# Delta-rule sequences: a 64x64 map per chunk made ahead of the chain, outputs taken from whole pairs

## The chip, the cores and the metric

The kernel runs on one core of a Trainium2 chip. The metric is the device time of one execution in microseconds (us), the median of three runs. The core has a matrix engine (TensorE, PE in the profile, with PEld for its weight loads), a vector engine (VectorE, DVE), an activation engine (ScalarE, ACT), GpSimd (POOL) and a queue that issues transfers (SyncE, SP). [...]

## The reference, cut to what matters

The program is a trunk of four layers over 1024 tokens with 1024 channels: gated convolution, diagonal state space, RWKV-7 time mixing, gated convolution. Only the third layer is touched. There, each of 16 heads carries a 64x64 state that is updated token by token:

```python
def _rwkv_step(state, inp):
    r_t, w_t, k_t, v_t, kk_t, a_t = inp
    sa = jnp.einsum("bhvk,bhk->bhv", state, -kk_t)
    state = (state * w_t[:, :, None, :] + sa[..., None] * (kk_t * a_t)[:, :, None, :]
             + v_t[..., None] * k_t[:, :, None, :])
    out = jnp.einsum("bhvk,bhk->bhv", state, r_t)
    return state, out
```

The outputs are normalised per head, get a bonus term, are gated by silu(z) and go through `w_out`.

## The kernel before, in words

**Tiling.** The layer treats the tokens in two halves of 512 (`h`), and the channels in eight blocks of 128 (`m`), two heads to a block. A unit is one pair (m, h): two heads, 512 tokens, eight chunks of 64 tokens. All large products (`sp`, `op`, lines 326 to 328) are split into three products of 128x128 by 128x512.

**The parts of a unit.** `use_k` and `use_r` turn the products for k and r into scaled tiles. `prep` (line 1960) makes the 64x64 products inside each chunk (`s`, line 1982), transposes the keys (`kbtp`, `kbt`) and makes the values that do not need the state (`wps`, into `uv`). `tsolve` (line 2024) inverts the unit triangular 64x64 system of each chunk on VectorE alone, in eight steps of three instructions (`tv` line 2048, `td` line 2053, `ti` line 2054). `join` (line 2057) completes the inverse (`tt`) with small products (`zp`, `tp`) and multiplies it into the keys (`a2`, line 2097). `seq` (line 2105) is the chain over the eight chunks:

- the bank `p1` is opened with `tt` times `uv` (line 2122), 16 small products a unit;
- for each chunk, one 128x128 product of the state with `ra` (line 2131) gives both this chunk's correction (64 rows) and, in the other 64 rows, the part of its outputs that the old state makes;
- ScalarE copies the correction into `uv` (line 2132);
- a second 128x128 product with `kbt` (line 2137) gives the update, of which VectorE uses the two diagonal 64x64 blocks, one instruction each (line 2140);
- after four chunks the outputs are completed with `scr` (line 2147) and copied into `o` (line 2150).

Then the outputs are normalised, transposed (`otp`, line 2176) and stored.

**What sets the order.** `rwkv_layer` writes units m = 0 to 7 of a half one after the other. Unit m's own k and r work is interleaved, by generators, with `tsolve` of unit m-1 and `seq` of unit m-2. A scheduler that knows priorities (`PS`, `PT`, `PJ` for `seq`, `tsolve` and `join`/`prep`) then fixes each engine's order. Behind the eighth unit of the first half come two products for z of the second half, the second half's small products (`pwa`, line 1640) and its z and v work; behind the eighth unit of the second half comes the output product (`op`). In these two places there is no next unit, and the last `tsolve`, `join` and `seq` have less beside them.

The state tile is 128x128 with zeros off the diagonal blocks. In `paux`, two PSUM banks under the name `aux` serve all short products; `pseq` holds one bank `sq` and two `p1`.

Of the kernel before, what the change touches and what calls it, by code (L numbers as in the profile page):

```python
# [15 lines left out]
P = 128  # L16
# [1581 lines left out]
def rwkv_layer(S, X, bg, l, last, nxt):  # L1598
# [9 lines left out]
    dST = dram_list(S, "dST", [P, P])  # L1608
# [313 lines left out]
def inner_setup(S, rg, T_):  # L1922
# [179 lines left out]

    gn, bn = S.vec[("lnx_g",)], S.vec[("lnx_b",)]

    def seq(m, h, R, dVT, dST, dBV, dZ, dY):
        st = rg.tile([P, P], F32, tag="state", name="state", bufs=2)
        if h == 0:
            G.memset(st, 0.0)
        else:
            nc.sync.dma_start(st, dST[m][:])  # L2110
        ot = rg.tile([P, HT], F32, tag="o", name="o", bufs=2)
        o4 = ot.rearrange("p (c s) -> p c s", c=4)

        def bank(ph):

            p1 = S.pseq.tile([P, 2, 2, P], F32, tag="p1", name="p1", bufs=2)
            nc.tensor.matmul(p1[:, 0, 0, 0:2], S.ident, zero, start=True, stop=False, skip_group_check=True)
            for c2 in range(2):
                for hd in range(2):
                    for w in range(2):  # L2120
                        rb, cs = rows_b[w], slice(hd * 64, hd * 64 + 64)
                        nc.tensor.matmul(p1[rb, w, c2, cs], R.tt[rb, 2 * (2 * ph + c2) + hd, :],
                                         R.uv[w][rb, 2 * ph + c2, cs], start=False, stop=False, skip_group_check=True)
            return p1
        p1s = [bank(0)]
        for c in range(8):
            w, c2, ph = c % 2, c // 2, c // 4
            rb = rows_b[w]
            uv = R.uv[w][:, c2, :]
            p1 = p1s[ph][:, w, c2 % 2, :]  # L2130
            nc.tensor.matmul(p1, R.ra[:, c, :], st, start=False, stop=False, skip_group_check=True)  # L2131
            SC.copy(uv[rb, :], p1[rb, :])  # L2132
            yield
            if c == 2:
                p1s.append(bank(1))
            p2 = sq("p2")
            last = nc.tensor.matmul(p2[:, 0:P], R.kbt[c // 4][:, c % 4, :], uv, start=True, stop=True)  # L2137
            for hd in range(2):
                cs = slice(hd * 64, hd * 64 + 64)
                V.scalar_tensor_tensor(st[cs, cs], st[cs, cs], R.pc[cs, c:c + 1], p2[cs, cs], ALU.mult, ALU.add)  # L2140
            if c % 4 == 3:
# [7 lines left out]
                for w in range(2):  # L2149
                    SC.copy(o4[rows_k[w], 2 * ph:2 * ph + 2, :], p1s[ph][rows_k[w], w])  # L2150
# [62 lines left out]
```

## Time and profile before

| what | value |
|---|---|
| median of three runs | 2815.74 us (2814.3 to 2817.0) |
| the profiled execution's own time | 2819.03 us |
| its span | 2817.1 us |
| PE, PEld busy | 2673.0 us (95%), 2119.2 us (75%) |
| DVE, ACT, POOL busy | 2009.8 us (71%), 1168.8 us (41%), 644.9 us (23%) |
| mean granted TensorE clock | 0.966 |
| instructions | 40692 |

The span is the time from the first to the last profiled instruction; the execution's own time is 1.9 us longer. A busy PE counts each product from its start to its modelled end, and products overlap; how many PE can do in a microsecond is read from the distance between starts, not from the busy share. Line numbers such as L2140 are those of the kernel before; in the changed kernel the lines from 2103 on are new.

### The profile page before, as it was taken

To read this page: it belongs to the slowest core of one execution; us is meant where nothing else is said; L and a number is where in the kernel's file an instruction comes from. 1 tells how busy PE (TensorE), PEld (TensorE's weight loads), DVE (VectorE), ACT (ScalarE), POOL (GpSimd) and SP (SyncE) were. 2 spreads that over 40 slices of the span, in tenths; PEclk is the share of its full clock that TensorE was granted. 3 is DMA by queue.
4 is the path that set the end of the run, shared out by engine and by line. 5 is a ranking of instruction groups with operands and counts; after the bars stand their busy time and mean duration, and the time that the engine had idled before them with its cause. 6 is when DMAs were issued, how large, how long until landed. Compare 5 with 4: busy or idle time off the path is not lost.

```text
span 2817.1 us, 40692 instructions
## 1 busy us (share of the span) xinstructions
PE 2673.0 (95%) x14939; PEld 2119.2 (75%) x14939; DVE 2009.8 (71%) x3584; ACT 1168.8 (41%) x2243; POOL 644.9 (23%) x696
## 2 busy tenths in 40 slices
PE   8999999999999999899899899888889999999998
PEld 6887888778887878677677567666668777887887
DVE  6787865477657446887887776888866678877544
ACT  3333332242135223666565475555433343224332
POOL 1143422221115132203243110333222211111000
PEclk9999999999999999999996799999799999999999
DMA  5333321347774233473222245223324433324511
GB/s 169 99 97 98 94 76 58 92 146 211 217 237 157 90 101 102 134 227 120 77 95 91 60 163 168 76 85 93 100 91 135 139 115 116 101 72 131 172 64 38
DMA packets 463129, 331.56 MB, mean 118 GB/s; under 512 B 49449, under 2 KB 398929, under 8 KB 462929
## 3 DMA queue, kind: packets, MB, share of 16 engines
q1 hardware_dynamic: 462928, 328.96, 38.5%
q8 instruction: 118, 1.93, 0.3%
q14 instruction: 83, 0.67, 0.1%
HBM read 250.77 MB, written 77.59 MB: 117 GB/s over the span
## 4 chain that ended last, share of the span: by engine, by line
PE 71%; DVE 15%; issue 4%; ACT 4%; DMA 3%; POOL 3%; SPq 0%; DVEq 0%; POOLq 0%; ACTq 0%
PE op L327 3%; PE op L326 3%; PE op L328 3%; PE gp L328 3%; PE gp L327 3%; PE gp L326 3%; PE sp L326 2%; PE sp L327 2%; PE sp L328 2%; PE qa L506 2%; PE qa L507 2%; PE qa L508 2%; DVE tv L2048 2%; PE zp L326 2%; PE zp L328 2%
## 5 line engine op out<-in xcount | busy, mean ns | idle before, releaser
L299 DVE TENSOR_TENSOR wl<-wraw,wh 128x1024 fp32r<-128x1024 f32 x255 | 332.6, 1304 | 217.0 <-ACT wh L298 213.5
L298 ACT CAST wh<-wraw 128x1024 fp32r<-128x1024 f32 x255 | 267.4, 1049 | 519.0 <-PE gp L327 185.9
L905 POOL TENSOR_TENSOR ln_s<-ln_s,rp 128x512 f32<-128x512 f32 x42 | 60.3, 1435 | 209.9 <-DVE rp L901 209.9
L2140 DVE SCALAR_TENSOR_TENSOR state<-state,pc,p 64x64 f32<-64x64 f32 x256 | 70.8, 277 | 39.7 <-PE p L2137 35.5
L2048 DVE TENSOR_TENSOR tv<-ti,mi 128x128 f32<-128x128 f32 (+3 forms) x128 | 97.1, 759 | 2.5
L2131 PE MATMUL p<-state,ra 128*128 128x128 f32 x256 | 65.2, 341 | 31.3 <-DVE state L2140 31.0
L2131 PEld LDWEIGHTS p<-state,ra 128*128 128x128 f32 x256 | 45.2, 213 | 54.8 <-DVE state L2140 49.2
L2132 ACT COPY uv<-p 64x128 f32<-64x128 f32 x128 | 33.3, 260 | 122.2 <-PE p L2131 121.0
L920 POOL TENSOR_TENSOR rp<-r_0h,r_0l 128x512 f32<-128x512 f32 x24 | 36.5, 1548 | 180.9 <-PE op L327 180.2
L328 PE MATMUL gp<-r_0h,wl 128*128 128x512 f32 x192 | 77.2, 402 | 0.0
L327 PE MATMUL gp<-r_0l,wh 128*128 128x512 f32 x192 | 76.8, 400 | 0.0
L326 PE MATMUL gp<-r_0h,wh 128*128 128x512 f32 x192 | 76.6, 399 | 0.0
L326 PE MATMUL gp<-r_1h,wh 128*128 128x512 f32 x192 | 76.4, 398 | 0.0
L328 PE MATMUL gp<-r_1h,wl 128*128 128x512 f32 x192 | 76.0, 396 | 0.2 <-DVE wl L299 0.2
L327 PE MATMUL gp<-r_1l,wh 128*128 128x512 f32 x192 | 75.5, 393 | 0.0
L2137 PE MATMUL p<-uv,kbt 128*128 128x128 f32 x256 | 66.2, 344 | 8.7 <-ACT uv L2132 8.6
L1982 PE MATMUL s<-ra,kb 64*128 64x128 f32 x512 | 71.6, 302 | 1.0 <-ACT scr L1988 0.9
L2137 PEld LDWEIGHTS p<-uv,kbt 128*128 128x128 f32 x256 | 44.9, 210 | 36.6 <-ACT uv L2132 31.3
L1982 PEld LDWEIGHTS s<-ra,kb 64*128 64x128 f32 x512 | 61.3, 202 | 13.4 <-ACT scr L1988 2.9
L1991 POOL TENSOR_TENSOR scr<-scr,mask 128x512 f32<-128x512 f32 x32 | 45.9, 1435 | 70.2 <-ACT scr L1988 70.0
L327 PE MATMUL sp<-xs0l,wh 128*128 128x512 f32 x128 | 55.0, 430 | 1.9 <-DVE xs0l L195 1.9
L1710 POOL COPY pc<-pt 128x8 f32<-128x8 f32 x16 | 5.5, 342 | 222.0 <-ACT pt L1707 222.0
(851 smaller groups left out, 8734.7 us busy)
## 6 DMA issues: line engine op xcount, KB each, us to landing
wraw<-in_conv_w_in_dram SPq DMA_DIRECT2D x84, 512.0 KB
wraw<-in_rwkv_w_rkvz_dram SPq DMA_DIRECT2D x64, 512.0 KB
wraw<-in_ple_gate_dram SPq DMA_DIRECT2D x56, 512.0 KB
wraw<-in_conv_w_out_dram SPq DMA_DIRECT2D x24, 512.0 KB
xt<-xd SPq DMA_DIRECT2D x48, 256.0 KB
wraw<-in_ssm_w_in_dram SPq DMA_DIRECT2D x21, 512.0 KB
xd<-rp SPq DMA_DIRECT2D x40, 256.0 KB
wraw<-in_rwkv_w_out_dram SPq DMA_DIRECT2D x16, 512.0 KB
```

What stands on the lines that cost most here:

```text
L298: nc.scalar.copy(wh, raw)
L299: nc.vector.tensor_tensor(wl, raw, f32(wh[:]), ALU.subtract)
L326: nc.tensor.matmul(ps, lh, xh, start=(n == 0), stop=False)
L327: nc.tensor.matmul(ps, lh, xl, start=False, stop=False)
L328: nc.tensor.matmul(ps, ll, xh, start=False, stop=(n == kt - 1))
L506: nc.tensor.matmul(ps, wh[:, k0 + k, :], xh, start=first and k == 0, stop=False, skip_group_check=True)
L905: nc.gpsimd.tensor_tensor(s, s, rs, ALU.add)
L1982: nc.tensor.matmul(pss[hd][:, c * P:(c + 1) * P], kb[rows, 2 * c + w, :], ra[rows, 2 * c + w, :], start=True, stop=True)
L2048: V.tensor_tensor(tv, ti[:, b:8, 4 * b:4 * b + 4].unsqueeze(2).to_broadcast([P, n, c, 4]), mi[:, 4 * b:4 * b + 4, 0:c].rearrange("p q c -> ...
L2131: nc.tensor.matmul(p1, R.ra[:, c, :], st, start=False, stop=False, skip_group_check=True)
L2137: last = nc.tensor.matmul(p2[:, 0:P], R.kbt[c // 4][:, c % 4, :], uv, start=True, stop=True)
L2140: V.scalar_tensor_tensor(st[cs, cs], st[cs, cs], R.pc[cs, c:c + 1], p2[cs, cs], ALU.mult, ALU.add)
```

## The change

`join` gets two more stages. The inverse `tt` is also multiplied into the transposed keys (`at`) and into the values (`u0`), and the result is multiplied with `kbt` (`gt`): a 64x64 map of each chunk and head, kept where `ant` stood. In `seq` all eight chunks' updates that do not need the state are accumulated into one bank `pd` beforehand (line 2145); a chunk of the chain is then one 64x64 product for each head with the state (line 2151) and one VectorE instruction over both heads (line 2153). The state after every chunk is kept (`sv`, 9 x 64 columns, 128 partitions). The products with `ra` (line 2169, K = 64, 64 columns, one for each head and chunk) now only feed the bank `p1`, which is opened with an identity product of `uv` (line 2164); the corrections are copied into `uv` four times a unit, and the outputs are completed with `scr` (line 2182) for the whole unit at once. The transposes at the end (`otp`) take an `aux` bank.

```diff
-    dST = dram_list(S, "dST", [P, P])
+    dST = dram_list(S, "dST", [P, CH])
...
+        pa, pu = aux("at"), aux("u0")
+        for dst, src in ((pa, lambda w, c2, cs: an[rows_b[w], c2, cs]),
+                         (pu, lambda w, c2, cs: R.uv[w][rows_b[w], c2, cs])):
+            for c2 in range(4):
+                for hd in range(2):
+                    for w in range(2):
+                        rb, cs = rows_b[w], slice(hd * 64, hd * 64 + 64)
+                        nc.tensor.matmul(dst[rb, c2 * P + hd * 64:c2 * P + hd * 64 + 64], tt[rb, 2 * c2 + hd, :],
+                                         src(w, c2, cs), start=True, stop=True)
+        SC.copy(R.ant, pa)
+        for w in range(2):
+            SC.copy(R.uv[w][rows_b[w]].rearrange("p a b -> p (a b)"), pu[rows_b[w], :])
+        yield
+        pg = [aux("gt"), aux("gt")]
+        for c2 in range(4):
+            for hd in range(2):
+                for w in range(2):
+                    rb, cs = rows_b[w], slice(hd * 64, hd * 64 + 64)
+                    nc.tensor.matmul(pg[w][cs, c2 * CH:(c2 + 1) * CH], an[rb, c2, cs],
+                                     R.kbt[c2 // 2][rb, (2 * c2 + w) % 4, cs], start=True, stop=True)
+        for w in range(2):
+            SC.copy(R.ant[:, w * 256:(w + 1) * 256], pg[w][:, 0:256])
+        yield
...
-        st = rg.tile([P, P], F32, tag="state", name="state", bufs=2)
+        sv = rg.tile([P, 9, CH], F32, tag="state", name="state", bufs=2)
...
-            nc.tensor.matmul(p1, R.ra[:, c, :], st, start=False, stop=False, skip_group_check=True)
-            SC.copy(uv[rb, :], p1[rb, :])
-            yield
-            if c == 2:
-                p1s.append(bank(1))
-            p2 = sq("p2")
-            last = nc.tensor.matmul(p2[:, 0:P], R.kbt[c // 4][:, c % 4, :], uv, start=True, stop=True)
-            for hd in range(2):
-                cs = slice(hd * 64, hd * 64 + 64)
-                V.scalar_tensor_tensor(st[cs, cs], st[cs, cs], R.pc[cs, c:c + 1], p2[cs, cs], ALU.mult, ALU.add)
...
+        pd = sq("pd")
+        clear(pd[:, 0:2])
+        for c in range(8):
+            for cs in heads:
+                nc.tensor.matmul(pd[cs, c * CH:(c + 1) * CH], R.kbt[c // 4][:, c % 4, cs], R.uv[c % 2][:, c // 2, cs],
+                                 start=False, stop=False, skip_group_check=True)
+        gt = R.ant.rearrange("p (w c k) -> p w c k", w=2, c=4)
+        yield
+        for c in range(8):
+            for cs in heads:
+                nc.tensor.matmul(pd[cs, c * CH:(c + 1) * CH], gt[cs, c % 2, c // 2, :], sv[cs, c, :],
+                                 start=False, stop=True, skip_group_check=True)
+            V.scalar_tensor_tensor(sv[:, c + 1, :], sv[:, c, :], R.pc[:, c:c + 1], pd[:, c * CH:(c + 1) * CH],
+                                   ALU.mult, ALU.add)
             yield
...
+        for w in range(2):
+            for hd in range(2):
+                nc.tensor.matmul(p1[hd][rows_b[w], :, w, :], S.ident[rows_b[w], rows_b[w]], R.uv[w][rows_b[w], :, heads[hd]],
+                                 start=False, stop=False, skip_group_check=True)
+        yield
+        for c in range(8):
+            for hd in range(2):
+                nc.tensor.matmul(p1[hd][:, c // 2, c % 2, :], R.ra[heads[hd], c, :], sv[heads[hd], c, :],
+                                 start=False, stop=False, skip_group_check=True)
...
+        for w in range(2):
+            for hd in range(2):
+                SC.copy(R.uv[w][rows_b[w], :, heads[hd]], p1[hd][rows_b[w], :, w, :])
+        yield
+        for c2 in range(4):
+            for hd in range(2):
+                for w in range(2):
+                    nc.tensor.matmul(p1[hd][rows_k[w], c2, w, :], R.scr[w][:, c2, hd, :], R.uv[w][:, c2, heads[hd]],
+                                     start=False, stop=True, skip_group_check=True)
+        for w in range(2):
+            for hd in range(2):
+                SC.copy(o4[rows_k[w], :, heads[hd]], p1[hd][rows_k[w], :, w, :])
...
-        ps = sq("otp")
+        ps = aux("otp")
```

How the engines' orders move is shown at three places. In these rows a name is the tile written, then the tiles read; a row's last number is the shape written, and a product that stands once in the order is two rows of the profile.

First, PE in the middle of a unit of the second half (unit 4), with the chain of an earlier unit in it. Before, one chunk after the other:

```order
L1759 MATMUL pb<-kpl,c_ones_r 128x512
L2131 MATMUL p_17709<-state,ra 128x128
L328 MATMUL sp<-xs0h,wl 128x512
L326 MATMUL sp<-xs0h,wh 128x512
L2137 MATMUL p_17762<-uv,kbt 128x128
L1982 MATMUL s_17964<-ra,kb 128x128 x4
L327 MATMUL sp<-xs0l,wh 128x512
L2131 MATMUL p_17709<-state,ra 128x128
L328 MATMUL sp<-xs0h,wl 128x512
L326 MATMUL sp<-xs0h,wh 128x512
L2137 MATMUL p_17768<-uv,kbt 128x128
L2147 MATMUL p_17709<-uv,scr 64x64 x8
```

Now, in the same unit:

```order
L2151 MATMUL pd<-state,ant 64x64 x2
L2169 MATMUL p_18475<-state,ra 128x64
L2169 MATMUL p_18476<-state,ra 128x64
L327 MATMUL sp<-xs1l,wh 128x512
L328 MATMUL sp<-xs1h,wl 128x512
L2151 MATMUL pd<-state,ant 64x64 x2
L2169 MATMUL p_18475<-state,ra 128x64
L2169 MATMUL p_18476<-state,ra 128x64
L326 MATMUL sp<-xs1h,wh 128x512
L2151 MATMUL pd<-state,ant 64x64 x2
```

A chunk was two products with two or three large ones after each; it is now four smaller ones in two shapes, with one or two large ones after them, and all eight chunks stand within some 40 rows.

Second, VectorE at the same place. Before, the two state updates of a chunk stand between the steps of `tsolve`:

```order
L2048 TENSOR_TENSOR tv<-ti,mi 128x288
L1735 TENSOR_TENSOR kk<-kk,prn 128x512
L2140 SCALAR_TENSOR_TENSOR state<-state,pc,p_17269 64x64 x2
L2053 TENSOR_REDUCE td<-tv 128x72
L1738 TENSOR_TENSOR kb<-kk,ga 128x4x2x64
L2054 TENSOR_TENSOR ti<-ti,td 128x3x24
L2048 TENSOR_TENSOR tv<-ti,mi 128x320
L2140 SCALAR_TENSOR_TENSOR state<-state,pc,p_17304 64x64 x2
L2053 TENSOR_REDUCE td<-tv 128x80
```

Now they stand close together behind most of `tsolve`:

```order
L2048 TENSOR_TENSOR tv<-ti,mi 128x128
L2153 SCALAR_TENSOR_TENSOR state<-state,pc,pd 128x64
L2053 TENSOR_REDUCE td<-tv 128x32
L2054 TENSOR_TENSOR ti<-ti,td 128x8x4
L2153 SCALAR_TENSOR_TENSOR state<-state,pc,pd 128x64 x2
L1735 TENSOR_TENSOR kk<-kk,prn 128x512
L2153 SCALAR_TENSOR_TENSOR state<-state,pc,pd 128x64
L1738 TENSOR_TENSOR kb<-kk,ga 128x4x2x64
L2153 SCALAR_TENSOR_TENSOR state<-state,pc,pd 128x64 x2
L299 TENSOR_TENSOR wl<-wraw,wh 128x1024
L1751 TENSOR_TENSOR ra<-sp,pt 128x4x128
```

The updates have one instruction or none between them, and what needs the outputs (`rs_t`, lines 1592 to 1595) follows two instructions later.

Third, VectorE at the end of the first half, around the last unit's transpose `mi` (line 1999). Before, the chain of unit 5 still runs behind it, between the second half's `mix` and `xs3l`:

```order
L1999 STREAM_TRANSPOSE mi<-dg 128x1024
L2140 SCALAR_TENSOR_TENSOR state<-state,pc,p_13858 64x64 x2
L2053 TENSOR_REDUCE td<-tv 128x80
L195 TENSOR_TENSOR xs3l<-mix,xs3h 128x512
L2054 TENSOR_TENSOR ti<-ti,td 128x5x16
L1570 SCALAR_TENSOR_TENSOR mix<-x_3_14093,vec_174,mix 128x512
L2140 SCALAR_TENSOR_TENSOR state<-state,pc,p_13893 64x64 x2
L2048 TENSOR_TENSOR tv<-ti,mi 128x288
```

Now unit 6's `tt` follows at once:

```order
L1999 STREAM_TRANSPOSE mi<-dg 128x1024
L195 TENSOR_TENSOR xs3l<-mix,xs3h 128x512
L2063 STREAM_TRANSPOSE tt<-ti 128x32x8 x2
L2068 STREAM_TRANSPOSE t_14603<-tt 128x256
L2037 TENSOR_TENSOR tp<-mi 128x12x16
L195 TENSOR_TENSOR xs3l<-mix,xs3h 128x512
L2040 TENSOR_TENSOR mi<-mi,tp 128x4x3x16
```

Unit 5's chain and the rest of unit 6's `tsolve` now stand ahead of the last `mi`, and so do most of the `mix` and `xs3l` that stood behind it.

More of the change, by code (lines that the diff above doesn't have):

```diff
@@ L2121, in bank @@
                         rb, cs = rows_b[w], slice(hd * 64, hd * 64 + 64)
[L2122 to L2125, printed above, removed]
-        for c in range(8):
[L2127 to L2132, printed above, removed]
-            yield
-            if c == 2:
-                p1s.append(bank(1))
-            p2 = sq("p2")
-            last = nc.tensor.matmul(p2[:, 0:P], R.kbt[c // 4][:, c % 4, :], uv, start=True, stop=True)
-            for hd in range(2):
-                cs = slice(hd * 64, hd * 64 + 64)
-                V.scalar_tensor_tensor(st[cs, cs], st[cs, cs], R.pc[cs, c:c + 1], p2[cs, cs], ALU.mult, ALU.add)
-            if c % 4 == 3:
-                with S.tc.issue_after(last.ins):
-                    for k in range(2):
-                        for hd in range(2):
-                            for w in range(2):
-                                cs = slice(hd * 64, hd * 64 + 64)
-                                nc.tensor.matmul(p1s[ph][rows_k[w], w, k, cs], R.scr[w][:, 2 * ph + k, hd, :],
-                                                 R.uv[w][:, 2 * ph + k, cs], start=False, stop=True, skip_group_check=True)
-                for w in range(2):
-                    SC.copy(o4[rows_k[w], 2 * ph:2 * ph + 2, :], p1s[ph][rows_k[w], w])
@@ new lines, in join, with seq, clear @@
+        for w in range(2):
+            SC.copy(R.ant[:, w * 256:(w + 1) * 256], pg[w][:, 0:256])
+        yield
+    gn, bn = S.vec[("lnx_g",)], S.vec[("lnx_b",)]
+    def seq(m, h, R, dVT, dST, dBV, dZ, dY):
+        sv = rg.tile([P, 9, CH], F32, tag="state", name="state", bufs=2)
+        if h == 0:
+            G.memset(sv[:, 0, :], 0.0)
+        else:
+            nc.sync.dma_start(sv[:, 0, :], dST[m][:])
+        heads = [slice(hd * 64, hd * 64 + 64) for hd in range(2)]
+        def clear(cols):
+            nc.tensor.matmul(cols, S.ident, zero, start=True, stop=False, skip_group_check=True)
+        pd = sq("pd")
+        clear(pd[:, 0:2])
+        for c in range(8):
+            for cs in heads:
[9 more added lines that the diff above has]
+                                   ALU.mult, ALU.add)
```

21 lines of the change are left out of this document (8 added, 13 removed).

## The prediction

> **What bounds the kernel now.** I read the page first, for the span and the groups that the change removes, then the chain of waits for where each unit starts, then windows, waits and the order in time of the stage that holds those groups.
>
> ```profile
> span 2817.1 us, 40692 instructions
> L2140 DVE SCALAR_TENSOR_TENSOR state<-state,pc,p 64x64 f32<-64x64 f32 x256 | 70.8, 277 | 39.7 <-PE p L2137 35.5
> L2131 PE MATMUL p<-state,ra 128*128 128x128 f32 x256 | 65.2, 341 | 31.3 <-DVE state L2140 31.0
> L2132 ACT COPY uv<-p 64x128 f32<-64x128 f32 x128 | 33.3, 260 | 122.2 <-PE p L2131 121.0
> ```
>
> There are 256 rows of L2140, 16 in each of 16 units, and 256 rows of L2131, two for each of 128 chunks. A chunk's chain is PE, ACT, PE, DVE, and each of the three engines is seen waiting for another. Whether that costs time depends on the stage. The transpose `mi` occurs once in a unit and marks it:
>
> ```profile
> 1401.87 1.91 DVE mi L1999
> 1553.07 2.02 DVE mi L1999
> 1821.17 1.93 DVE mi L1999
> 1972.13 1.89 DVE mi L1999
> ```
>
> From 1821.17 to 1972.13 lie four equal units of the second half, 37.7 us each; from 1401.87 to 1553.07 four of the first half, the last two already near its end. The windows are these stretches, then the ends of the two halves (columns: length, busy us and instructions of PE, PEld, DVE, ACT, POOL, granted clock, DMA share, GB/s):
>
> ```profile
> 1821.17:1972.13 150.96, 130.42 (x1355) 99.71 (x1354) 134.44 (x304) 87.80 (x251) 54.12 (x55) 0.99 0.29 87
> 1401.87:1553.07 151.20, 138.89 (x1270) 108.22 (x1269) 127.78 (x295) 88.14 (x245) 55.69 (x58) 0.83 0.30 93
> 1553.07:1626.10 73.03, 60.69 (x530) 40.01 (x528) 53.76 (x123) 37.21 (x107) 9.53 (x14) 0.79 0.18 50
> 1972.13:2064.45 92.32, 80.77 (x788) 63.44 (x786) 72.64 (x166) 45.84 (x136) 19.07 (x21) 0.80 0.32 99
> ```
>
> In the even units VectorE is busy 33.6 of 37.7 us: it is the bound there, and only 4.1 us a unit are left to waits. At the ends it idles 19.3 of 73.0 and 19.7 of 92.3 us, and PE runs at a granted clock of 0.79 and 0.80 against 0.99. The even units have work and little waiting; the ends have waiting.
>
> **What PE can take in the even units.** Its busy time overlaps itself, so I take the distance between starts:
>
> ```profile
> 1924.15 0.50 PE L327 MATMUL sp<-xs0l,wh 128*128 128x512 f32 x1
> 1924.49 0.39 PE L2131 MATMUL p<-state,ra 128*128 128x128 f32 x2
> 1924.63 0.48 PE L328 MATMUL sp<-xs0h,wl 128*128 128x512 f32 x1
> 1924.96 0.40 PE L326 MATMUL sp<-xs0h,wh 128*128 128x512 f32 x1
> 1925.23 0.49 PE L2137 MATMUL p<-uv,kbt 128*128 128x128 f32 x2
> 1925.65 0.69 PE L2147 MATMUL p<-uv,scr 128*64 128x64 f32 x16
> 1926.26 1.16 PE L1982 MATMUL s<-ra,kb 64*128 64x128 f32 x8
> ...
> 1928.46 1.71 PE L1982 MATMUL s<-ra,kb 64*128 64x128 f32 x16
> 1930.10 0.49 PE L2137 MATMUL p<-uv,kbt 128*128 128x128 f32 x2
> 1930.34 0.48 PE L326 MATMUL sp<-xs0h,wh 128*128 128x512 f32 x1
> 1930.65 0.39 PE L327 MATMUL sp<-xs0l,wh 128*128 128x512 f32 x1
> 1930.88 0.40 PE L328 MATMUL sp<-xs0h,wl 128*128 128x512 f32 x1
> ```
>
> A large product takes 0.23 us (1930.65 to 1930.88). L2131 and the large one after it take 0.47 (1924.49 to 1924.96), so a chain product takes 0.24. 16 rows of the 128x64 shape take 0.61, 16 rows of the 64x128 shape 1.64 (0.10 each). A change of shape costs extra: L2137 to L2147 is 0.42 where 0.24 is usual, so 0.18; a large product into L2131 behind another shape 0.34 where 0.23 is usual, so about 0.1. The 64x64 shape is read from the chain of waits:
>
> ```profile
> 1342.87 1.08 PE a L2097 x32
> 1343.94 1.12 PE p L2122 x28
> ```
>
> So 32 rows, sixteen products, take 1.08. With the counts of the same four units, of which the largest are
>
> ```profile
> L1982 PE MATMUL s<-ra,kb 64*128 64x128 f32 x128 | 16.1, 285 | 0.0
> L2137 PE MATMUL p<-uv,kbt 128*128 128x128 f32 x64 | 15.1, 319 | 0.0
> L2131 PE MATMUL p<-state,ra 128*128 128x128 f32 x64 | 14.4, 307 | 11.2 <-DVE state L2140 11.2
> L328 PE MATMUL sp<-xs1h,wl 128*128 128x512 f32 x32 | 14.0, 438 | 0.0
> ```
>
> (six groups of 32 large ones, 192 x 0.23 = 44; L1982 13; L2131 and L2137 15; the 64x64, 32x32, 128x64 and transposing groups about 42), PE needs some 114 of the 151 us, 28.5 a unit. PE has 9 us a unit to spare, VectorE 4.
>
> **The change part by part, in an even unit.** *VectorE.* Sixteen L2140 at 0.277 become eight of 128x64. Such an instruction's length is bounded below by the old one of 64x64 (64 elements on each partition in both) and above by two of them; I take 0.28, as the column count is the same. 4.4 becomes 2.2: 33.6 falls to 31.4.
>
> *PE, added.* `at` is 32 rows of the 64x64 shape: 1.08; `gt` the same: 1.08; `u0` is what the opening of the bank was (L2122), nothing. `pd` is 32 rows of 128x64: 1.2. L2151 is 32 rows of 64x64: 1.1. L2169 is 32 rows of 64x128 with half the columns of L1982: between 1.6 and 3.3; I take 2.8, nearer to L1982, whose weights have the same shape. The identity products, eight rows of 256 columns, lie between 32-row packing and half a large product each, 0.3 to 0.9: 0.7. One more clearing product: 0.1. Each chunk is one trip out of the large shape, through two small ones, and back, 0.1 + 0.18 at the least: between nothing (hidden by packing) and 2.2 for eight; I take 1.5. Removed: 16 chain products, 3.8. The sum is +5.8, between +2.6 and +7.1. PE needs 34.3 us, within 31.1 and 35.6.
>
> [...]
>
> *ScalarE.* Away go eight L2132 (2.1) and four copies into `o`; added are one 128x512, two 64x512, two 128x256 and eight 64x256 copies, some 2 us more in all on 22 of 37.7: nothing, covered by 15 us of idle time. SyncE's transfer of the state halves: nothing.
>
> *The chain.* A chunk loses the copy and one product. Its trip is now one instruction of VectorE (0.28), a product pair (0.49 until its end) and two handoffs, about 0.9 if nothing stands between. But in the new order the eight updates stand almost alone on VectorE, and PE has one or two large products (0.23 to 0.47) and L2169 between: about 1.2 a chunk, 9 to 10 us, of which VectorE fills some 6 (eight updates, `kk`, `kb` and the last steps of `tsolve`). So 3 to 4 us of new idle time stand against 2.2 of work saved and these waits of the four even units, of which the change removes the second and fourth:
>
> ```profile
> DVE n L1725 <- PE pss L1716: 4.4, 4, 1.1
> DVE state L2140 <- PE p L2137: 2.9, 4, 1.7
> DVE tp L2037 <- PE tp L2084: 2.6, 4, 0.7
> DVE ra L1751 <- PE p L2131: 2.6, 4, 0.9
> ```
>
> That is 1.4 a unit. Together -3.6 and +3.5: I take **no change in the nine even units** (five of the second half, four of the first), within -2 (VectorE sets the pace still) and +3 (PE does) a unit, -18 to +27.
>
> *The ends.* Here the chain's length itself is waited for. At the end of the first half unit 6's eight chunks run alone with `tsolve` of unit 7:
>
> ```profile
> 1584.20 0.27 DVE L2140 SCALAR_TENSOR_TENSOR state<-state,pc,p 64x64 f32<-64x64 f32 x1 [0.86 <-PE p L2137]
> ...
> 1609.51 0.59 DVE L2140 SCALAR_TENSOR_TENSOR state<-state,pc,p 64x64 f32<-64x64 f32 x2 [3.32 <-PE p L2137]
> ```
>
> They take 25.9 us (1584.20 to 1610.10), 3.2 a chunk, and hold up `tsolve` of unit 7, which stands between them on VectorE, and with it the last `join`. The longest of a step's three instructions has this row of the page:
>
> ```profile
> L2048 DVE TENSOR_TENSOR tv<-ti,mi 128x128 f32<-128x128 f32 (+3 forms) x128 | 97.1, 759 | 2.5
> ```
>
> With its two shorter followers I estimate 1.35 us a step, 10.8 for eight. In the new order a chunk stands between these steps and needs 1.2 itself, so the two go side by side in some 14: 12 saved. Unit 5's chunks, which filled 1555 to 1570 between the second half's first `mix`, go ahead into the idle time of the unit before (its share of the 23.4 us in the second window): 10 more, if that time takes them all; I take 9. The two new stages of `join` cost twice a product group and a copy, 2 x (1.1 + 0.6), about 3, before the chain of unit 7 and the second half's small products behind it. 12 + 9 - 3 = **-18**. The end of the second half has as much idle time on VectorE and three units' updates (6.6 us) to save, but the output products already fill PE in part and must still be done; I take two thirds, **-12**.
>
> Sum: -18 - 12 + 0 = -30 on the profiled execution's 2819.0, which is 2789; the median is 3.3 below that execution, so **2786**.
>
> **The rivals.** *VectorE keeps the pace everywhere.* If the small shapes pack as `a` does and switching is hidden, PE needs 31, and each even unit falls by 2: -18 - 30, 2768. For it: 9 us a unit to spare on PE. Against it: PE and VectorE would both be at 31 and wait for each other in turn.
>
> *PE becomes the bound and the change is slower.* At +7.1 PE needs 35.6; it leaves these waits of PE in the four even units, 2.2 each, and the updates standing alone add 2: 40, +2.5 in nine units and 5 lost again at the ends.
>
> ```profile
> PE kbtp L2006 <- POOL kb L2001: 5.1, 4, 1.6
> PE otp L2176 <- POOL o L2169: 3.8, 4, 1.0
> ```
>
> The point is where PE's need passes the old 33.6 of VectorE by more than 1. With only half the gain at the ends: +22 + 5 - 15, 2828. For it: the trips between shapes. A second price goes the same way: the granted clock, 0.99 in the even units, was 0.79 where few large products are left, and in the new order `at`, `u0`, `gt` and `pd` follow one another with few large ones.
>
> [...]
>
> *Nothing happens.* The chain was hidden after all and what it frees at the ends goes into waits for weights or for ScalarE, as at the first end already:
>
> ```profile
> DVE mix L1570 <- ACT mix L1569: 8.9, 2, 6.2
> ```
>
> That leaves the even units' 0 and an eighth of the ends: 2812.
>
> **How the numbers follow.** My forecast (ends gained, even units level) has 0.52, VectorE keeps the pace 0.20, PE the bound 0.18, nothing 0.10. A measurement of this kernel tells about 0.2%, 5.6 us, from no change. Of the forecast and the first rival nearly all is faster by more; of "nothing" a third: faster 0.73, within 0.2% 0.10, slower 0.17. The forecast's own range is 2768 to 2804; to leave out no more than 2 in 10 it runs from 2758 (the first rival with better ends) to 2822 (most of the second).
>
> **What would show it.** Right: between the `mi` marks the even units stay at 37 to 39 us, PE's busy share there rises, VectorE's falls to about 31.4 of busy time; the wait of the copy L2132 (121 us) is gone and no wait of `uv` of that size takes its place; the stretch from the last `mi` of the first half to the second half's small products shrinks from 60 us (1553 to 1613) to 45 or less, and the granted clock at the ends rises. Wrong: even units of 40 us with VectorE waiting for `pd` (PE the bound), or of 36 (VectorE still), or updates of 128x64 that take much more than 0.28.

## The result and the profile after

The changed kernel takes 3082.9 us (median of four, 3074.7 to 3089.4), the kernel before 2816.4 beside it: a ratio of 1.094, with a 95% interval of 1.091 to 1.097. Forecast were 2786, at most 2822. The change is slower by some 267 us.

The page of the changed kernel, with the groups that answer to L2140 and L2131 of before, and the new wait of the transposes:

```profile
span 3087.7 us, 45120 instructions
L2153 DVE SCALAR_TENSOR_TENSOR state<-state,pc,pd 128x64 f32<-128x64 f32 x128 | 35.7, 279 | 170.3 <-PE pd L2151 169.7
L2169 PE MATMUL p<-state,ra 64*128 64x64 f32 x512 | 88.3, 409 | 0.0
L2210 PE MATMUL otp<-ident,o 128*128 128x128 f32 x64 | 16.0, 389 | 49.9 <-POOL o L2203 49.8
```

VectorE's part did what was forecast: 128 updates of 0.279 us where 256 of 0.277 stood. But VectorE now waits 170 us for `pd`, where it waited 36 for L2137.

Where the time lies is seen in windows. The first two rows of each kernel run from the first `mi` of the first half to its eighth, and from there to the first `mi` of the second half; the next two are the same of the second half, up to the end of the span. Before:

```profile
1308.20:1553.00 244.80, 223.92 (x2049) 174.70 (x2050) 212.68 (x474) 141.17 (x375) 88.90 (x91) 0.88 0.28 89
1553.00:1764.00 211.00, 189.82 (x1124) 139.76 (x1122) 150.88 (x281) 128.06 (x279) 24.63 (x29) 0.89 0.41 129
1764.00:2014.10 250.10, 216.65 (x2097) 169.10 (x2097) 218.05 (x484) 138.65 (x375) 89.79 (x87) 0.92 0.29 89
2014.10:2817.10 803.00, 770.39 (x3729) 621.07 (x3727) 543.52 (x875) 288.19 (x503) 106.01 (x94) 0.98 0.34 106
```

After, and below them the four units that answer to the even ones of the prediction's first window:

```profile
1307.20:1688.70 381.50, 338.93 (x2985) 252.13 (x2986) 207.89 (x469) 163.19 (x423) 89.67 (x97) 0.73 0.20 61
1688.70:1888.50 199.80, 181.00 (x1294) 136.16 (x1292) 124.55 (x220) 117.96 (x239) 19.20 (x24) 0.89 0.41 129
1888.50:2275.30 386.80, 350.11 (x2993) 258.99 (x2993) 200.00 (x460) 156.44 (x412) 88.88 (x91) 0.71 0.19 60
2275.30:3087.70 812.40, 784.63 (x3934) 629.08 (x3932) 523.05 (x834) 281.44 (x474) 103.55 (x91) 0.97 0.33 103
...
1975.00:2219.40 244.40, 217.60 (x1875) 158.43 (x1873) 112.82 (x267) 94.08 (x255) 52.34 (x56) 0.68 0.16 51
```

Each half's units lost 136.7 us (381.5 - 244.8 and 386.8 - 250.1). The stretch behind the first half gained 11.2, the end lost 9.4. Of the 273 us in both halves, 24 lie in the two last units (from the seventh `mi` of a half to its eighth: 45.6 became 55.7, and 42.0 became 55.9). The rest lies in what the forecast called the even units, at "no change": 61.1 us each (244.4 / 4) where 37.7 stood, VectorE busy for 28.2 of them, and PE at a granted clock of 0.68 where it had 0.99.

One unit in the order of time, PE alone, from the second chunk of the chain to the next unit's `s`:

```profile
1483.64 0.48 PE L2151 MATMUL pd<-state,ant 64*64 64x64 f32 x4
1484.05 0.69 PE L2169 MATMUL p<-state,ra 64*128 64x64 f32 x4
1484.67 0.79 PE L327 MATMUL sp<-xs1l,wh 128*128 128x512 f32 x1
1485.27 0.63 PE L328 MATMUL sp<-xs1h,wl 128*128 128x512 f32 x1
1485.82 0.48 PE L2151 MATMUL pd<-state,ant 64*64 64x64 f32 x4
...
1495.98 0.48 PE L2151 MATMUL pd<-state,ant 64*64 64x64 f32 x4
...
1500.29 1.85 PE L2182 MATMUL p<-uv,scr 128*64 128x64 f32 x32
1502.08 0.50 PE L328 MATMUL sp<-xs1h,wl 128*128 128x512 f32 x1
1503.15 0.65 PE L2138 MATMUL p<-zero,ident 128*128 128x2 f32 x4 [0.58 <-ACT o L2186]
1508.20 1.11 PE L2210 MATMUL otp<-ident,o 128*128 128x128 f32 x4 [4.40 <-POOL o L2203]
...
1510.18 2.47 PE L1982 MATMUL s<-ra,kb 64*128 64x128 f32 x16
```

Two things are to be seen. First, a chunk takes 2.2 us (1483.64 to 1485.82), PE is at work for all of it, and a large product takes 0.55 to 0.60 us, where the prediction's rows had 0.23: the granted clock is at half from 1481.4 to 1501.9. Second, `s` of the next unit stands behind the whole chain, behind L2182 and behind `otp`, which waits 4.4 us for the normalised `o`. Before, `s` stood between the chunks (the prediction's row at 1926.26, ahead of L2137 and L2131). The next unit's `prep` no longer runs beside the chain.

### The profile page after: what moved, and what is told of

It is laid out like the page before. It is cut to its first block, busy times and chain, and to the rows that moved or that the text cites. A ratio compares the mean times of both kernels' runs of the same rounds, so it can differ in the third digit from the quotient of the medians.

```text
span 3087.7 us, 45120 instructions
## 1 busy us (share of the span) xinstructions
PE 2924.5 (95%) x17147; PEld 2289.2 (74%) x17147; DVE 1941.1 (63%) x3456; ACT 1192.0 (39%) x2259; POOL 637.0 (21%) x696
## 4 chain that ended last, share of the span: by engine, by line
PE 75%; DVE 8%; issue 7%; ACT 4%; POOL 3%; DMA 2%; SPq 0%; DVEq 0%; POOLq 0%; ACTq 0%
PE op L328 3%; PE op L327 3%; PE op L326 3%; PE sp L326 3%; PE gp L328 3%; PE gp L327 3%; PE gp L326 3%; PE p L2169 3%; PE sp L327 3%; PE sp L328 2%; PE zp L326 2%; PE zp L327 2%; PE zp L328 2%; PE pd L2151 2%; PE qa L507 2%
## 5 line engine op out<-in xcount | busy, mean ns | idle before, releaser
L2153 DVE SCALAR_TENSOR_TENSOR state<-state,pc,pd 128x64 f32<-128x64 f32 x128 | 35.7, 279 | 170.3 <-PE pd L2151 169.7
L2169 PE MATMUL p<-state,ra 64*128 64x64 f32 x512 | 88.3, 409 | 0.0
L1757 POOL TENSOR_TENSOR kpl<-kp,kph 128x512 fp32r<-128x512 f32 x16 | 20.7, 1293 | 301.6 <-ACT kph L1756 224.4
L2048 DVE TENSOR_TENSOR tv<-ti,mi 128x128 f32<-128x128 f32 (+3 forms) x128 | 79.1, 618 | 3.4
L1982 PEld LDWEIGHTS s<-ra,kb 64*128 64x128 f32 x512 | 61.5, 251 | 23.2 <-ACT yt L2213 8.0
L2169 PEld LDWEIGHTS p<-state,ra 64*128 64x128 f32 x512 | 63.6, 277 | 19.4 <-issue 5.7
L920 POOL TENSOR_TENSOR rp<-r_0h,r_0l 128x512 f32<-128x512 f32 x24 | 37.5, 1592 | 167.4 <-PE op L327 167.1
L2151 PEld LDWEIGHTS pd<-state,ant 64*64 64x64 f32 x512 | 34.7, 184 | 50.2 <-issue 32.7
L2210 PE MATMUL otp<-ident,o 128*128 128x128 f32 x64 | 16.0, 389 | 49.9 <-POOL o L2203 49.8
L326 PE MATMUL sp<-xs1h,wh 128*128 128x512 f32 x128 | 63.1, 493 | 0.0
L327 PE MATMUL sp<-xs1l,wh 128*128 128x512 f32 x128 | 63.0, 492 | 0.0
```

Of the source, the lines that this page charges most:

```text
L326: nc.tensor.matmul(ps, lh, xh, start=(n == 0), stop=False)
L327: nc.tensor.matmul(ps, lh, xl, start=False, stop=False)
L920: (eng or nc.gpsimd).tensor_tensor(rs, f32(rh[:]), f32(rl[:]), ALU.add)
L1982: nc.tensor.matmul(pss[hd][:, c * P:(c + 1) * P], kb[rows, 2 * c + w, :], ra[rows, 2 * c + w, :], start=True, stop=True)
L2048: V.tensor_tensor(tv, ti[:, b:8, 4 * b:4 * b + 4].unsqueeze(2).to_broadcast([P, n, c, 4]), mi[:, 4 * b:4 * b + 4, 0:c].rearrange("p q c -> ...
L2151: nc.tensor.matmul(pd[cs, c * CH:(c + 1) * CH], gt[cs, c % 2, c // 2, :], sv[cs, c, :], start=False, stop=True, skip_group_check=True)
```

## The experiments

Three theories: **A (bank)**, `otp` in the ring of two `aux` banks ties the next unit's `prep` to the end of the chain; **B (clock)**, the small shapes bring PE's granted clock down, and that costs the time; **C (work)**, PE's products with the trips between shapes are simply longer than forecast.

### The bank of the transposes

```diff
-        ps = aux("otp")
+        ps = sq("otp")
```

> The changed kernel with one line undone: the transposes `otp` take the bank `sq` again and not one of the two `aux` banks. Theory A (bank): the two `aux` banks go round in the written order, so with `otp` among them the products `s` of the next unit's `prep` cannot begin before the chain of the unit before has ended and been normalised; the half granted clock of the units follows from that. Then the undone line gives back most of the 267 us: units of 38 to 44 us, PE's granted clock in them 0.9 or more, 2790 to 2880. Theory B (clock): the chain's small shapes alone bring the half clock; then only PE's wait at `otp` goes, some 4 us in each of 11 units: 3020 to 3050, the units at a clock of about 0.7. Theory C (work and trips between shapes on PE): as B, 3030 to 3060, since the same products remain.

Measured: 2949.4 us (2927.1 to 2962.1), 1.047 of before (1.041 to 1.052), mean clock 0.945. The line gives back 134 of 267 us: more than B or C allow, less than A said. And the last line of the change alone, on the kernel before:

```diff
-        ps = sq("otp")
+        ps = aux("otp")
```

> The kernel before with nothing changed but that `otp` takes an `aux` bank: the last line of the change alone, with the old chain. Theory A: this line alone makes the even units serial: units of 50 to 60 us at a low granted clock, 2980 to 3150. Theories B and C: the old chain's large shapes and its old work remain, so at most a few waits at `otp`: 2810 to 2860.

Measured: 2991.9 us, one execution (before: 2812.7). This line alone costs 179 us, with the old chain and its large shapes. In its profile PE's order shows the same place:

```profile
1971.27 1.12 PE L2147 MATMUL p<-uv,scr 128*64 128x64 f32 x16
1973.24 0.59 PE L2117 MATMUL p<-zero,ident 128*128 128x2 f32 x2 [0.84 <-ACT o L2150]
1977.14 1.11 PE L2176 MATMUL otp<-ident,o 128*128 128x128 f32 x4 [3.32 <-POOL o L2169]
...
1979.13 2.29 PE L1982 MATMUL s<-ra,kb 64*128 64x128 f32 x16
```

`s` needs an `aux` bank; the two banks are handed out in the written order, and `otp` stands ahead of it there. So A holds as a cause, and the low clock came here without a new product: these units ran at 0.71 with the old ones.

```profile
1932.70:2154.20 221.50, 182.33 (x1319) 138.79 (x1319) 121.31 (x300) 90.23 (x252) 51.59 (x55) 0.71 0.18 57
```

With `otp` in `sq` (the first run), 137 us are left. Windows of single units of it:

```profile
1379.40:1419.90 40.50, 40.50 (x459) 29.94 (x457) 30.08 (x68) 23.47 (x64) 14.53 (x15) 0.99 0.26 81
1470.20:1506.40 36.20, 35.27 (x435) 26.32 (x437) 27.25 (x64) 18.66 (x55) 11.69 (x14) 1.00 0.23 68
1419.90:1470.20 50.30, 49.62 (x494) 36.47 (x488) 31.39 (x68) 25.71 (x70) 13.68 (x17) 0.80 0.22 70
1891.40:1947.40 56.00, 52.25 (x429) 38.30 (x428) 28.50 (x64) 20.73 (x61) 14.52 (x16) 0.62 0.16 49
```

PE stands still for 3.8 us or less in each of them, so there is little waiting left to remove. Of the twelve units that count here (six in each half, without the short first one), three run at full clock and take 36 to 44 us; the other nine have half clock in them and take 45 to 59. And `s` is back between the chunks, where the new products' durations at full clock can be read:

```profile
1408.19 0.33 PE L2151 MATMUL pd<-state,ant 64*64 64x64 f32 x4
1408.45 0.44 PE L2169 MATMUL p<-state,ra 64*128 64x64 f32 x4
1408.82 0.66 PE L1734 MATMUL prn<-ident,rnb 128*128 128x128 f32 x4
...
1412.14 1.16 PE L1982 MATMUL s<-ra,kb 64*128 64x128 f32 x8
1413.23 0.33 PE L2151 MATMUL pd<-state,ant 64*64 64x64 f32 x4
```

A chunk's L2151 takes 0.26 us until L2169 starts (forecast 0.14), L2169 takes 0.37 (forecast 0.35).

### The clock, taken alone

To the changed kernel, `otp` left in `aux`, two products of zeros are added behind each chunk's second L2151 (`last`). They accumulate into the outputs' banks `p1`, so they change no result. For that these banks are opened ahead of the chain, and the products with `ra` come behind it; this holds for all three runs. In the first run `zr` is 512 columns of zeros in float32r; the second has 2 columns in plain f32 instead, the third the same 512 columns with weights of 32x32:

```diff
-                nc.tensor.matmul(pd[cs, c * CH:(c + 1) * CH], gt[cs, c % 2, c // 2, :], sv[cs, c, :],
+                last = nc.tensor.matmul(pd[cs, c * CH:(c + 1) * CH], gt[cs, c % 2, c // 2, :], sv[cs, c, :],
...
+            with S.tc.issue_after(last.ins):
+                for _ in range(2):
+                    nc.tensor.matmul(p1[c % 2].rearrange("p a b c -> p (a b c)"), S.rw.ones_r, zr, start=False, stop=False,
+                                     skip_group_check=True)
```

> The changed kernel with `otp` in `aux` as it is, and two products of 128x128 by 512 columns of zeros behind each chunk's L2151, which add nothing to the bank `p1` that they write (16 a unit, 256 in all; the products with `ra` then stand behind the chain). At 0.235 us each they are 3.8 us of work a unit at full clock. Theory B: they keep the clock full, and the products that took twice their time at half clock take it no more: 2900 to 3000. Theory A: the unit stays serial, the chain gets longer by what the zeros take, though at a better clock: 3000 to 3100. Theory C: work is added: 3120 to 3190.

> As the run with the zeros, but each added product has 2 columns, not 512: it costs little and is no activity, and only the order stays like it (the products with `ra` behind the chain and not in it). Theory C: 14 fewer trips between shapes in a unit: 3000 to 3050. Theories A and B: nothing of the cause is touched: 3050 to 3100. The difference between the two runs is what the zeros' activity does: below 0 by B, above +30 by C.

> As the run with 256 products of 128x128 by 512 columns of zeros on the changed kernel (3036.6 us, mean clock 0.953), but each of these products uses 32 rows and 32 columns of the array, not 128 and 128: the same 512 columns are streamed, over a sixteenth of the array (the sum they add stays zero). If the clock follows how long PE is busy, the result is as there, 3010 to 3060 and a clock of about 0.95. If it follows how much of the array works, it is as in the run with 2 columns (3144.4 us, 0.911) or later still by the products' own time: 3130 to 3230 and a clock of 0.92 or less.

Measured, one execution each:

| added product, 256 of them | time | mean granted clock |
|---|---|---|
| 128x128 weights, 512 columns | 3036.6 us | 0.953 |
| 128x128 weights, 2 columns | 3144.4 us | 0.911 |
| 32x32 weights, 512 columns | 3153.2 us | 0.908 |

Two of the added groups in the pages, the large zeros and the small ones:

```profile
L2164 PE MATMUL p<-zr,c_ones_r 128*128 128x512 f32 x256 | 101.5, 478 | 0.0
L2164 PE MATMUL p<-zr,c_ones_r 32*32 32x512 f32 x256 | 114.0, 533 | 0.0
```

The large zeros make the program 46 us faster than the changed kernel and 108 faster than the 2-column products, though they are work. Streaming the same 512 columns through a sixteenth of the array brings nothing of that: 116.6 us slower, although at full clock, from start to start, the small products take nearly as long as the large ones (4.6 and 4.8 us a unit). In the order of the table the twelve units take 55.6, 61.5 and 63.4 us on average; weighted with the granted clock they are 46.4, 44.9 and 44.2, so the two slower runs have no more to do, they do it at a lower clock. So the granted clock is a cause of its own here, and for nearly the same time of PE it went with how much of the array worked: a mean of 0.953 with the zeros over 128x128, of 0.908 with the same columns over 32x32.

The expectations held in part. The difference of -108 is what B said and C excludes, but 3036.6 lies in the range of A (the unit stays in line, at a better clock) and not in B's, and 3144.4 lies above every range. The reason is a price: the 2-column products are not nearly free. Counted from start to start at full clock they take 3.9 us a unit. So the pair compares nearly equal time of PE, for 2 columns and for 512, at a mean clock of 0.911 and 0.953; but it tells nothing on trips.

### Work and area

The products of one shape are kept together (`otp` in `sq`; nothing else but the order changes): the 16 products of `a` behind the last `tp` product (`last`), the outputs' identity products behind the last product that opens `pd` (`opened`).

```diff
-        for c2 in range(4):
+        with S.tc.issue_after(last.ins):
+            for c2 in range(4):
...
-                nc.tensor.matmul(p1[hd][rows_b[w], :, w, :], S.ident[rows_b[w], rows_b[w]], R.uv[w][rows_b[w], :, heads[hd]],
-                                 start=False, stop=False, skip_group_check=True)
+                with S.tc.issue_after(opened.ins):
+                    nc.tensor.matmul(p1[hd][rows_b[w], :, w, :], S.ident[rows_b[w], rows_b[w]], R.uv[w][rows_b[w], :, heads[hd]],
+                                     start=False, stop=False, skip_group_check=True)
```

> The changed kernel with `otp` in `sq`, and with the products of one shape kept together: `a` behind all of `tp` in `join`, and the identity products behind the opening of `pd` (order only, nothing is left out). In the run with `otp` in `sq` alone, PE's work in a unit, counted at full clock, was 39.3 us, where 34.3 was predicted; 1.0 of it was `a`, 0.5 `tp`, 0.6 `pd` and 0.9 the identity products beyond the durations predicted for them, for the trips between shapes. Theory C (what is left is PE's work, with the trips): 3 us less in a unit, and since PE is the bound there, 35 to 60 us less in all: 2885 to 2915. Theory B (what is left is the half clock): the same shapes in longer runs without large products between: little or no gain, 2920 to 2970, the units' clock as before or lower.

Measured: 2959.6 us (2953.0 to 2964.9), 1.050 (1.048 to 1.052). PE's need, counted from start to start at full clock over twelve units, fell from 39.3 to 36.6 us a unit, and the time did not fall. (Such a count is an estimate, good to about 1 us, as it depends on which short gaps go into it.) C as the whole of the rest is refuted. Then the outputs' products over both heads again, with the states of both heads on a diagonal (128x128, zeros beside it), and each bank of outputs copied out behind its four chunks:

```diff
-                nc.tensor.matmul(p1[hd][:, c // 2, c % 2, :], R.ra[heads[hd], c, :], sv[heads[hd], c, :],
-                                 start=False, stop=False, skip_group_check=True)
...
+            nc.tensor.matmul(p1[ph][:, w, k, :], R.ra[:, c, :], sv[:, c, :], start=False, stop=False, skip_group_check=True)
+            for cs in heads:
+                V.scalar_tensor_tensor(sv[cs, c + 1, cs], sv[cs, c, cs], R.pc[cs, c:c + 1], pd[cs, c * CH:(c + 1) * CH],
+                                       ALU.mult, ALU.add)
```

> As the grouped one, and the products with `ra` are 128x128 over both heads again (the state is kept as 9 blocks of 128 columns with zeros off the diagonal, so that its update is two instructions of 64x64 as before the change), and each half of the chunks completes its outputs at once. The small product of the chain and everything in `join` remain. PE: 32 rows of L2169 at 0.11 to 0.16 become 16 at about 0.13: 1.5 to 3 us less in a unit, one shape less in each chunk; VectorE 2.2 us more. Theory B: eight products a unit have their whole area again, the clock comes back over 0.9 in the units and with it most of the rest: 2790 to 2850. Theory C: 1.5 to 3 us of some 36 in 12 units: 20 to 35 less than the grouped one.

Measured: 2848.4 us (2844.7 to 2851.5), 1.011 (1.009 to 1.012), mean clock 0.977. That is 111 us less than the grouped one, for a need of PE that fell by 1.1 us a unit only (36.6 to 35.5, so 13 us in twelve units), and with two updates a chunk on VectorE. A unit of the grouped one:

```profile
1421.70:1468.80 47.10, 44.23 (x455) 33.35 (x454) 31.34 (x67) 22.07 (x57) 13.72 (x16) 0.75 0.20 63
```

Two of the wide one:

```profile
1409.20:1449.00 39.80, 35.91 (x472) 26.88 (x471) 32.74 (x75) 23.45 (x66) 14.38 (x16) 1.00 0.26 83
1449.00:1486.90 37.90, 35.14 (x435) 26.88 (x435) 32.68 (x75) 23.17 (x63) 12.70 (x15) 1.00 0.27 85
```

What differs is the clock. The wide run also copies its outputs out earlier, so the gain could come from fewer waits. It does not: over the twelve units PE idles 2.9 us a unit, where it idled 3.4, and the length weighted with the granted clock is 37.8 us, where it was 38.2, while the length itself is 40.7 where it was 49.2. B's numbers held (2790 to 2850), C's did not. The last cross of the two, wide and not grouped, with `otp` in `aux`:

> The changed kernel with `otp` left in `aux` and nothing grouped, but with the products with `ra` as 128x128 over both heads, a state of 9 blocks of 128 columns and two updates of 64x64 a chunk (the wide form of the run that gave 2848 with `otp` in `sq` and grouping). If the bank and the area are two separate prices: the serial units of `otp` in `aux` remain, as in the kernel before with `otp` in `aux` (2992): 2970 to 3030. If the area alone mattered: 2840 to 2900.

Measured: 3027.6 us, one execution, mean clock 0.940. Bank and area are two prices, and they do not add up: the narrow outputs cost 55 us with `otp` in `aux`, where the units run partly at half clock anyway, and 101 to 111 with it in `sq`.

| | `otp` in `sq` | `otp` in `aux` |
|---|---|---|
| kernel before | 2816 | 2992 |
| new chain, wide outputs | 2848 (grouped) | 3028 |
| new chain, narrow outputs | 2949 (grouped: 2960) | 3083 |

### The forecast's own terms

VectorE's saving alone, on the kernel before (the state 128x64, one bank `p1` for each head):

```diff
-            nc.tensor.matmul(p1, R.ra[:, c, :], st, start=False, stop=False, skip_group_check=True)
+            for cs, t in zip(heads, p1):
+                nc.tensor.matmul(t[:, c2, w, :], R.ra[cs, c, :], st[cs, :], start=False, stop=False, skip_group_check=True)
...
-            last = nc.tensor.matmul(p2[:, 0:P], R.kbt[c // 4][:, c % 4, :], uv, start=True, stop=True)
-            for hd in range(2):
-                cs = slice(hd * 64, hd * 64 + 64)
-                V.scalar_tensor_tensor(st[cs, cs], st[cs, cs], R.pc[cs, c:c + 1], p2[cs, cs], ALU.mult, ALU.add)
+            for cs in heads:
+                last = nc.tensor.matmul(p2[cs, 0:CH], R.kbt[c // 4][:, c % 4, cs], uv[:, cs], start=True, stop=True)
+            V.scalar_tensor_tensor(st, st, R.pc[:, c:c + 1], p2[:, 0:CH], ALU.mult, ALU.add)
```

> The kernel before with the one update alone: the state is 128x64 (both heads over one another), a chunk has one VectorE instruction and not two, and for that L2131 and L2137 are one small product for each head (64x128 and 128x64, 64 columns; the first writes one bank for each head); no map, no new stage in `join`, `otp` in `sq` as before. First term of the forecast: VectorE has 2.2 us less in a unit of 37.7 that it paces: 1.5 to 2 us in nine units, 2795 to 2805. Theory B (area): these 16 products a unit work on half the area, the half clock appears in the even units and what VectorE saves is lost: 2830 to 2900. Theory C (trips between shapes on PE, some 3 us a unit where 4 to 8 are free): 2810 to 2825.

Measured: 2858.9 us (2848.6 to 2870.1), 1.016 (1.012 to 1.020), mean clock 0.953: slower, as by B. Its windows tell more:

```profile
1403.10:1441.10 38.00, 35.79 (x375) 25.60 (x376) 30.12 (x67) 21.58 (x63) 12.68 (x14) 1.00 0.26 85
1441.10:1479.10 38.00, 35.55 (x373) 24.92 (x371) 30.40 (x68) 22.87 (x69) 14.40 (x16) 1.00 0.29 89
1949.10:2000.30 51.20, 44.72 (x348) 33.69 (x348) 30.47 (x71) 21.92 (x67) 14.06 (x13) 0.59 0.20 63
```

The same three units in the kernel before:

```profile
1401.80:1440.40 38.60, 35.57 (x346) 26.61 (x346) 32.40 (x78) 21.95 (x63) 14.06 (x15) 1.00 0.32 98
1440.40:1479.10 38.70, 36.45 (x344) 27.45 (x343) 36.49 (x78) 23.24 (x64) 16.88 (x17) 0.94 0.27 88
1934.60:1972.00 37.40, 31.42 (x337) 23.89 (x335) 33.61 (x76) 22.07 (x64) 13.96 (x14) 1.00 0.29 87
```

In the first two VectorE is busy for 30.1 and 30.4 us where it was busy for 32.4 and 36.5, and the units take 38.0 where they took 38.6 and 38.7. So 2 to 6 us less of VectorE's work are worth 0.6 or 0.7. This run does not change VectorE's work alone, as PE's sixteen products became 32 small ones; that VectorE was not the bound before is therefore likely from it, and not shown. The third window is the other price: with sixteen products a unit cut to half the area, the clock there is 0.59 where it was 1.00.

The ends alone: the new form for the units m = 6 and 7 of each half, the old one (`seq` as in the kernel before) elsewhere, and `otp` in `sq` for all.

```diff
+NEW = (6, 7)
...
-    I.prep, I.tsolve, I.join, I.seq = prep, tsolve, join, seq
+    I.prep, I.tsolve, I.join = prep, tsolve, join
+    I.seq = lambda m, *a: (seq_n if m in NEW else seq)(m, *a)
```

> The kernel before, with the new form (map, `pd`, one update, whole pairs, `otp` in `sq`) for the units m = 6 and 7 of each half alone. The forecast's step on the ends: the chains of these units lie where PE and VectorE wait, and the shorter chain gains 18 and 12 us: 2780 to 2800. If the ends too are paced by PE at a low clock, the added products cost what the shorter chain saves: 2810 to 2840.

Measured: 2828.3 us (2823.3 to 2834.8), 1.004 (1.003 to 1.006): a small loss, not -30, and in the range of the other expectation. Its two end stretches take 211.6 and 810.6 us (before: 211.0 and 803.0). On VectorE, unit 6's chain and the `tt` of unit 7 that ends its `tsolve`:

```profile
1591.48 0.28 DVE L2236 SCALAR_TENSOR_TENSOR state<-state,pc,pd 128x64 f32<-128x64 f32 x1 [0.66 <-PE pd L2234]
...
1601.21 0.28 DVE L2236 SCALAR_TENSOR_TENSOR state<-state,pc,pd 128x64 f32<-128x64 f32 x1
...
1603.03 1.07 DVE L2064 STREAM_TRANSPOSE tt<-ti 128x256 f32<-128x256 f32 x2
```

Before, the two longest waits of that `tsolve` for the chain, and its `tt`:

```profile
1598.93 0.27 DVE L2140 SCALAR_TENSOR_TENSOR state<-state,pc,p 64x64 f32<-64x64 f32 x1 [1.87 <-PE p L2137]
...
1602.12 0.27 DVE L2140 SCALAR_TENSOR_TENSOR state<-state,pc,p 64x64 f32<-64x64 f32 x1 [0.71 <-PE p L2137]
...
1604.25 1.05 DVE L2063 STREAM_TRANSPOSE tt<-ti 128x256 f32<-128x256 f32 x2
```

Eight chunks take 10.0 us (1591.48 to the end of the update at 1601.21), 1.25 each, close to the forecast, and they took 25.9. But they begin 7.3 us later than before (1584.20), since `at`, `u0`, `gt` and the opening of `pd` stand ahead, and `tt` comes at 1603.0 where it came at 1604.2. The chain had held `tsolve` up for some 3.4 us before `tt` (0.86 at 1584.20, then 1.87 and 0.71), not for the 12 that the forecast wanted to save; the large step from 1605.59 to 1609.51 in the chain lies behind `tt`.

Last, whether the low clock in the ends of the kernel before is worth anything: zeros (128x128 by 384 columns, into columns of `sq` that nobody reads) behind each chunk's L2137, for m = 4 to 7; two a chunk in the first run, four in the second:

```diff
+            if m >= 4:
+                with S.tc.issue_after(last.ins):
+                    for _ in range(2):
+                        nc.tensor.matmul(p2[:, P:HT], S.rw.ones_r, zr[:, P:HT], start=True, stop=True)
```

> The kernel before, unchanged but for two products of 128x128 by 384 columns of zeros into the unused columns of the bank `sq` behind each chunk's L2137, for the units m = 4 to 7 of each half (128 products; their sums are never read). There PE ran at a granted clock of 0.79 to 0.84, and in the stretch from 1507 to 1553 almost wholly at half clock with PE at work for 41 of 45.6 us. Theory B (clock, as an effect of its own): the products that are at half clock there get faster by more than the zeros take: 10 to 35 us less, 2780 to 2805. Theory C: 128 products of 0.18 us are up to 23 us of work, partly in PE's waits: 2815 to 2840.

> As the run before this one with four such products behind each chunk, not two. Theory B: if two did not suffice to hold the clock in these stretches, four do: 2770 to 2805; if two did, four cost up to 20 us more than two. Theory C: 2835 to 2860.

Measured: 2830.4 us, 1.004 (1.003 to 1.006), and 2836.2, 1.008 (1.006 to 1.010). Both expectations of B were wrong. Before, the seventh unit of the first half:

```profile
1507.40:1553.00 45.60, 40.76 (x297) 33.54 (x298) 34.31 (x79) 22.81 (x65) 13.99 (x15) 0.51 0.28 91
```

The same unit with four zeros a chunk:

```profile
1509.20:1552.10 42.90, 32.73 (x317) 25.55 (x317) 37.20 (x88) 20.55 (x61) 12.63 (x14) 0.84 0.24 78
```

The clock came back from 0.51 to 0.84 and the unit got 2.7 us shorter, no more, with some 6 us of zeros in it; PE idles 10.2 us where it idled 4.8. So in this unit the half clock cost little, because PE was not what it waited for. No version of these was faster than the kernel before.

## Why the prediction was wrong, step by step

**Even units, "no change".** This is the step that failed, by some 23 us a unit, and it failed in three places.

*The edit that was costed at nothing.* The part on the change quotes `ps = aux("otp")` in the diff and gives it no term. It is the largest: 134 us in this kernel, 179 alone. What is queued behind the moved tile was not asked: behind `otp` in the ring of the two `aux` banks stands `s`, and behind that the whole next unit.

*The granted clock.* It was named, in the second rival, as "a second price" that "goes the same way", and no microsecond was put on it; the rival stood at 2828 without it. The runs give about 100 us for it in the new chain with `otp` in `sq` (111 from narrow to wide outputs, of which some 13 are PE's work). The three runs with added products show the area in it: with 512 columns of zeros over 128x128 of the array the mean clock was 0.953, over 32x32 it was 0.908, and with 2 columns over 128x128 0.911, where the changed kernel had 0.913. PE's busy share does not tell it: in the run with `otp` in `sq`, the unit at 1419.90 had PE busy for 49.6 of 50.3 us and a clock of 0.80.

*PE's sum.* +5.8, within +2.6 and +7.1, was +9.5 (29.8 to 39.3 us a unit, from start to start at full clock). `at` 1.0 and `gt` 1.1 were right (1.08 each). Too small were L2151 (1.1; 2.2), the identity products (0.7; 1.7), `pd` (1.2; 1.9) and L2169 (2.8; 3.6), for which, as trips between shapes, 1.5 had been set apart. The trips are the likely reason for `pd` and L2169: in the run with the large zeros, where each of these groups stands more together, they take 1.2 and 2.7, as forecast. Not counted at all were old products that the new order splits: `a` and `tp` rose from 1.4 to 3.0. But the trips were the cheapest of the three: without 2.7 us of them the time stayed.

**VectorE as the bound.** 33.6 of 37.7 us busy was read as "the bound there". With 2 to 6 us less of it, in the run with one update, a unit moved by 0.6 or 0.7. A share of 89% with waits on both sides does not name the bound, and the first rival (2768) fell with the forecast.

**VectorE's and ScalarE's terms** were right: 0.279 us an update against 0.28; ScalarE's additions cost nothing that was seen. VectorE's busy time in a unit fell further than 31.4, to 28.2 (the windows hold fewer instructions too).

**The chain.** "About 1.2 a chunk" holds in the run with the ends alone (10.0 us for eight). In the changed kernel it is 2.2 at half clock.

**The ends, -18 and -12.** They came out at -11.2 and +9.4, and the first of these is given back in the unit before it, which grew from 45.6 us to 55.7 (part of the 136.7), as the unit before the second end grew from 42.0 to 55.9. The mechanism was wrong: `tsolve` was held up by the chain for some 3.4 us only. In the run with the ends alone the chain's end moved by 8.6 us (1610.10 to 1601.49) while `tt` moved by 1.2. The joins' new stages, set at 3, and the opening of `pd` put off the chain of unit 6 alone by 7.3 us. In the wide version the ends do gain, 207.9 and 794.9 us against 211.0 and 803.0, some 11 of the 30.

**The rival "PE becomes the bound"** had the direction and named PE's work and the clock, at a chance of 0.18 and with a time 255 us too low. It did not have the bank, which is half of the loss, so in that half it had the direction by luck.

What stays open: how the last 30 us of the wide version split between PE's larger need (35.5 against 29.8) and what half clock is left in its units.

## What to carry to other kernels

When an edit moves a tile into another ring of buffers, cost it like a moved instruction: write down who takes the next buffer of that ring, and what it will now wait for. On PE, count a product twice, once by its time and once by the area of the array that it uses: in the run with one update, with sixteen products a unit cut to half the area, a unit ran at a granted clock of 0.59 that had 1.00 in the kernel before. In the new chain the lower clock cost some 100 us, where PE had hardly any waits, and little in a unit of the kernel before that waited for something else (2.7 us less as 0.51 became 0.84, with some 6 us of zeros in it). Before an engine is called the bound by its busy share, look for the waits on the other side, or take some of its work away and see.

## What the runs showed of the hardware

The granted clock of a unit did not go with PE's busy share:

| run, start of the unit | length | PE busy | granted clock |
|---|---|---|---|
| kernel before, 1934.60 | 37.40 us | 31.42 us (84%) | 1.00 |
| `otp` in `sq`, 1379.40 | 40.50 us | 40.50 us (100%) | 0.99 |
| `otp` in `sq`, 1419.90 | 50.30 us | 49.62 us (99%) | 0.80 |
| one update, 1949.10 | 51.20 us | 44.72 us (87%) | 0.59 |
| kernel before, 1507.40 | 45.60 us | 40.76 us (89%) | 0.51 |

Products of zeros raised it in two of the runs. Four of 128x128 by 384 columns behind each chunk of the kernel before, for m = 4 to 7, brought the last of these units from 0.51 to 0.84; two float32r ones of 128x128 by 512 columns behind each chunk of the changed kernel brought the mean clock from 0.913 to 0.953. With 512 columns over 32x32 it was 0.908, with 2 columns over 128x128 0.911. How much work of which area a unit needs for the full clock, these runs do not show. And sixteen products of 2 columns in plain f32 with full weights, each two rows of the profile, took 3.9 us of PE's time, counted from start to start at full clock, where sixteen float32r products of 512 columns took 4.8: four fifths, so they were no cheap filler here.
